# Turning the third and fourth bank of x in 32 by 32 blocks on VectorE and through DRAM

## The chip, the cores and the metric

The kernel runs on one core of a Trainium2 chip. The metric is the device time of one execution in microseconds (us). A core has TensorE (matmuls; the profile calls it PE, and PEld for its weight loads), VectorE (DVE), ScalarE (ACT), GpSimd (POOL) and SyncE (SP), which here only issues DMAs. Each engine works through its own queue in order.

## The reference, cut to what matters

One decoder block on x of 1 x 2048 x 1024 in fp32: a normed and modulated input, one wide projection, two branches (a recurrence and an attention in three window sizes), a merge and an output projection with the residual.

```python
h = rms_norm(x, g_norm[l]) * (1.0 + scale[:, None, :]) + shift[:, None, :]
proj = h @ w_in[l]
x_rnn, z_rnn, q, k, v, z_attn, g_r, g_a = jnp.split(proj, IN_SPLITS, axis=-1)
...
qh = apply_partial_rope(q.reshape(B, S, N_HEADS, HEAD_DIM), cos, sin)
kh = apply_partial_rope(k.reshape(B, S, N_HEADS, HEAD_DIM), cos, sin)
```

The change concerns how h comes to lie with its 1024 features on the partitions, as the matmuls of `proj` want it, for the second half of the rows.

## The kernel before

**Banks and halves.** The 2048 rows are four banks of 512; bank n holds four residues r = 0 to 3 of 128 rows each. Half f = 0 works on banks 0 and 1, half f = 1 on banks 2 and 3. The 1024 features are KT = 8 slices k of 128; KH = 4 slices make one operand half. A bank of x is loaded with rows on partitions (`load_x`, L541: two DMAs of 1 MB, each with two residues), normed (squares with a row sum, a reciprocal root, a scaling), and then *turned*: `turned` (L561) transposes, for one k, the four 128 x 128 pieces on TensorE into a PSUM tile, and `build` (L564) makes from it a high part (L571, ScalarE, with scale and shift by feature) and a low part (L578 and L166 or L169) of an operand. The split into high and low is there because every fp32 product is computed as three fp32r matmuls (L152).

**The products.** Two weight blocks of 128 columns make a pair; for a pair and the two banks of a half, `strassen` (L349) computes seven products of 12 matmuls of 128 x 512 (a *product* below) instead of eight, from sums of weights and sums of operands (B11, B21 from the even bank; B12, B22 from the odd one; T1 to T4 mixed). Their order is X(B11), the previous pair's V(B22), Z(T2), W(T3), V(T1), X(B21), Y(T4). X has two PSUM buffers, Z, W, V and Y one each. The X of a pair is copied by ScalarE to u1 (L385) before X(B21) adds into the same bank; VectorE adds u2 (L386) and u3 (L391) and evicts V and Y with a sum (`total`, L455).

**What sets the order.** Around the change the order on every engine is the order in which the code is written (`tc.manual_schedule()`). `prod` counts the products, and after the matmuls of product n, ahead of its eviction, `run_late` runs what `later(d, fn)` or `steps_after` have registered for it; so "at product d" is a place in the queue of each engine. Weights are loaded (L255, on SP), summed (L284 to L298, VectorE) and split (L160 ScalarE, L166 GpSimd) four products ahead.

**The rotated phase** of a half is the last of its projection: six pairs (rotated q, two plain, rotated k, two plain), 42 products; in the first half it runs from 571.16 to 688.75 us, product 16 at 611.96 us. The evictions there (L1118, L455) are scaled (L1123), rotated on VectorE and GpSimd (L1138, L1142, L1145) and stored to `kqT` by SP (L1150, L1182). In the first half `next_norm` (L1285) loads bank 2 at product 3, squares at 7 to 10 (L1293), takes the root at 11 and 12 (L173, L178 to L182), scales at 14 to 17 (L1297), and `next_even` (L1302) turns and builds its eight k's in the last two pairs. The turned x of bank 3 is made later, in the second half's values stage (`values_half(1)`): the load is issued at its start, `norm_x` (L545) norms it, and `build_odd` (L588) turns and builds B12 (tile b12h, b12l) and B22, then T1 to T4, while TensorE computes the values of bank 2.

## Time and profile before

| | |
|---|---|
| median of 3 runs | 2168.82 us (2168.06 to 2169.25) |
| profiled execution | 2169.86 us |
| its span | 2168.0 us |
| granted TensorE clock, mean | 0.998 |
| TensorE busy | 2138.5 us, 99% |
| VectorE, ScalarE, GpSimd busy | 1495.3, 1295.4, 1111.4 us |
| DMA | 521.39 MB, mean 240 GB/s |

All rows of the profile are of the one profiled execution. A row of a timeline gives the start and the duration in us, the engine, the line, the operation, out<-in by the program's names, shape and count, and in brackets the idle time of that engine just before and what ended it. "SPq" is SyncE's queue issuing DMAs. Matmuls overlap, so what one costs is read from the distance of starts.

### The profile page before, as it was taken

The numbers are of one execution on the slowest core, as the hardware profiler recorded it, in microseconds if no ns is written. First come the engines' busy times: TensorE is split into PE (matmuls) and PEld (weight loads), VectorE is DVE, ScalarE is ACT, GpSimd is POOL, SyncE is SP. The second block draws the span as 40 slices with busy tenths as digits, with TensorE's granted clock in tenths as the row PEclk, the third lists the DMA queues.
The fourth block names the chain that finished last, engine by engine and source line by source line (L and its number), as shares of the span: only waits on it lengthen the run. The fifth ranks groups of instructions, "written<-read, shape, count | busy, mean of one in ns | idle before, by whom it ended". The sixth has DMA issues, their size and how long they took to land.

```text
span 2168.0 us, 32583 instructions
## 1 busy us (share of the span) xinstructions
PE 2138.5 (99%) x10538; PEld 1788.4 (82%) x10539; DVE 1495.3 (69%) x2590; ACT 1295.4 (60%) x2591; POOL 1111.4 (51%) x868
## 2 busy tenths in 40 slices
PE   9999999999999999999999999999999999999998
PEld 6888788888888888888888887888888988878886
DVE  6759877768656725544446584677777787688887
ACT  5748668668644537557547522777877877444333
POOL 1467667677666322223224664466666564422444
PEclk9999999999999999999999999999999999999999
DMA  8467887886655378899996667889886777898553
GB/s 301 144 209 260 278 296 266 284 302 222 175 116 166 113 244 286 294 311 308 326 322 212 161 162 212 279 260 281 263 270 212 244 230 235 298 321 293 181 171 111
DMA packets 416431, 521.39 MB, mean 240 GB/s; under 512 B 107558, under 2 KB 282882, under 8 KB 415236
## 3 DMA queue, kind: packets, MB, share of 16 engines
q1 hardware_dynamic: 376244, 401.65, 59.6%
q10 hardware_dynamic: 34384, 99.78, 12.2%
q0 software_dynamic: 5632, 17.88, 2.5%
q8 instruction: 83, 1.36, 0.2%
q14 instruction: 88, 0.72, 0.1%
HBM read 332.02 MB, written 187.17 MB: 239 GB/s over the span
## 4 chain that ended last, share of the span: by engine, by line
PE 66%; DVE 6%; DMA 5%; ACT 2%; issue 2%; POOL 1%; SPq 0%; POOLq 0%; ACTq 0%; DVEq 0%
PE X L152 13%; PE V L152 13%; PE pj L152 9%; PE Z L152 7%; PE W L152 7%; PE Y L152 6%; PE sc L152 4%; PE o L152 4%; PE pg L152 1%; DMA fg<-mrT 1%; PE pT L1560 1%; DMA fg<-gaT 1%; PE pT L1573 1%; DVE ptl L169 1%; DVE yl L169 1%
## 5 line engine op out<-in xcount | busy, mean ns | idle before, releaser
L166 POOL TENSOR_TENSOR S<-R,S 128x512 fp32r<-128x512 f32 x192 | 295.3, 1545 | 170.1 <-ACT S L160 90.5
L152 PE MATMUL X<-T,S 128*128 128x512 f32 x1344 | 323.9, 390 | 1.5 <-ACT u L385 1.3
L152 PE MATMUL pj<-yh,S 128*128 128x512 f32 x896 | 324.8, 404 | 0.3 <-DVE S L169 0.3
L152 PE MATMUL V<-T,S 128*128 128x512 f32 x1344 | 324.3, 390 | 0.5 <-DVE ev L455 0.5
L152 PEld LDWEIGHTS X<-T,S 128*128 128x128 f32 x1344 | 251.8, 188 | 56.3 <-ACT u L385 2.8
L152 PEld LDWEIGHTS V<-T,S 128*128 128x128 f32 x1344 | 252.0, 188 | 54.4 <-ACT S L160 0.9
L166 POOL TENSOR_TENSOR S<-s,S 128x512 fp32r<-128x512 f32 x116 | 170.4, 1469 | 148.1 <-ACT S L160 112.1
L152 PEld LDWEIGHTS pj<-yh,S 128*128 128x128 f32 x896 | 168.7, 189 | 30.3 <-DVE S L169 1.3
L152 PE MATMUL pj<-yl,S 128*128 128x512 f32 x448 | 176.2, 393 | 0.5 <-POOL yl L166 0.3
L1475 ACT ACTIVATE pp<-pp,st 128x256 f32<-128x256 f32 (+3 forms) x256 | 133.6, 523 | 67.4 <-DVE st L1474 66.1
L160 ACT ACTIVATE S<-s 128x512 fp32r<-128x512 f32 x124 | 77.3, 624 | 143.7 <-DVE s L285 93.2
L152 PE MATMUL W<-T,S 128*128 128x512 f32 x672 | 161.7, 390 | 0.0
L152 PE MATMUL Y<-T,S 128*128 128x512 f32 x672 | 161.6, 390 | 0.0
L152 PE MATMUL Z<-T,S 128*128 128x512 f32 x672 | 161.4, 389 | 0.0
L160 ACT ACTIVATE S<-R 128x512 fp32r<-128x512 f32 x200 | 121.4, 622 | 59.0 <-issue 15.2
L169 DVE TENSOR_TENSOR ptl<-pT,pth 128x384 fp32r<-128x384 f32 (+1 forms) x160 | 97.9, 629 | 76.1 <-ACT pth L160 73.8
L152 PEld LDWEIGHTS W<-T,S 128*128 128x128 f32 x672 | 126.0, 188 | 26.9 <-issue 0.9
L152 PEld LDWEIGHTS Z<-T,S 128*128 128x128 f32 x672 | 126.2, 188 | 26.1
L152 PEld LDWEIGHTS Y<-T,S 128*128 128x128 f32 x672 | 126.1, 188 | 26.1
L974 DVE SCALAR_TENSOR_TENSOR xc<-xr,par,xc 128x512 f32<-128x512 f32 x96 | 103.7, 1080 | 57.2 <-ACT xc L968 54.9
L166 POOL TENSOR_TENSOR s<-R,s 128x512 fp32r<-128x512 f32 x32 | 43.1, 1346 | 189.0 <-ACT s L160 176.4
L1540 ACT ACTIVATE pp<-pp,M 128x256 f32<-128x256 f32 (+3 forms) x256 | 118.0, 523 | 9.9 <-DVE M L1663 9.9
(416 smaller groups left out, 4929.1 us busy)
## 6 DMA issues: line engine op xcount, KB each, us to landing
sD<-S ACTq DMA_DIRECT2D x140, 512.0 KB, 3.7
S<-sD SPq DMA_DIRECT2D x140, 512.0 KB, 5.5
S<-wD SPq DMA_DIRECT2D x82, 512.0 KB, 5.6
R<-in_w_in_dram SPq DMA_DIRECT2D x144, 256.0 KB, 3.4
wD<-s ACTq DMA_DIRECT2D x64, 256.0 KB, 5.6
kraw<-kqT SPq DMA_DIRECT2D x32, 384.0 KB, 5.2
T<-in_w_mod_dram SPq DMA_DIRECT2D x16, 512.0 KB, 9.1
vN<-ev SPq DMA_DIRECT2D x32, 256.0 KB, 2.8
```

Of the source, the lines that this page charges most:

```text
L152: nc.tensor.matmul(o, lhsT=l, rhs=r, start=st, stop=sp, **kw)
L160: nc.scalar.activation(o, i, AF.Copy)
L166: nc.gpsimd.tensor_tensor(o, i, h.bitcast(F32), ALU.subtract)
L169: return nc.vector.tensor_tensor(o, i, h.bitcast(F32), ALU.subtract).ins
L974: nc.vector.scalar_tensor_tensor(xc, xr[:, i : i + CH], cw(i), xc, ALU.mult, ALU.add)
L1475: nc.scalar.activation(pdst, pdst, AF.Exp, bias=m_, scale=-1.0, accum_out=l_)
L1540: nc.scalar.activation(pp, pp, AF.Copy, scale=w)
L1560: nc.tensor.transpose(pt[:, c0 + j * P : c0 + (j + 1) * P], pp[i][:, k * P : (k + 1) * P], ident)
L1573: nc.tensor.transpose(pt[:, c * P : (c + 1) * P], pp[:, half * P : (half + 1) * P], ident)
```

## The change

There is a DRAM scratch `xD`. In the first half's rotated phase `next_banks` replaces `next_norm`: it loads, norms and turns bank 3 (load at product 1, squares at 5 and 6, root at 7 and 8, scaling at 9 and 10, turning at 11 and 12) and then bank 2 (the same steps from product 12: load 12, squares 16 and 17, turning 22 and 23). `turn_rows` turns one k by four VectorE transposes of 128 x 128, which transpose each 32 x 32 block in place in its 4 x 4 grid, into an "hf" tile (two buffers), and stores that to `xD` by SP (256 KB). `load_turned` brings back four k's with four DMAs, so that the blocks come to lie at their transposed places, in runs of 128 numbers. Bank 2 is reloaded at products 25 and 26 and built without TensorE by `next_even`; bank 3 is reloaded at the start of the second half into the tile `hx` and built in `build_odd`, where strided views (`by_window`, `by_class`) undo the order in which the columns lie. `norm_x` for bank 3 in the second half is gone, and so are the 64 TensorE transposes of banks 2 and 3.

```diff
--- before.py
+++ after.py
@@ -117,6 +117,8 @@
     gateD = scratch("gateD", [1, D])
 
     tabD = scratch("tabD", [2, 2, 32, HALF])
+
+    xD = scratch("xD", [2, KT, P, CH])
 
     sD = scratch("sD", [REBUILT * 7, P, 2, KH, P])
 
@@ -578,6 +580,30 @@
             nc.vector.tensor_scalar(hf[:], pv, g, s, ALU.mult, ALU.add)
             (lo_dve if k % 3 == 0 else lo_pool)(hl[:, k % KH, :], hf[:], hh[:, k % KH, :])
 
+    by_class = lambda ap: ap.rearrange("p (r b a) -> p r b a", r=4, b=4)
+    by_window = lambda ap: ap.rearrange("p (b r a) -> p r b a", r=4, b=4)
+
+    def turn_rows(st, xs, n, k):
+
+        w = T(st, [P, CH], F32, "hf", bufs=2)
+        for r in range(4):
+            nc.vector.transpose(w[:].rearrange("p (t r a) -> p r t a", t=4, r=4)[:, r], xs[r][:, k * P : (k + 1) * P])
+        nc.sync.dma_start(xD[n % 2, k], w[:])
+
+    def load_turned(dst, n, kh):
+
+        src = xD[n % 2, kh * KH : (kh + 1) * KH].rearrange("k (b i) (t q) -> t i k b q", b=4, t=4)
+        for t in range(4):
+            nc.sync.dma_start(dst[t * 32 : (t + 1) * 32].rearrange("p k (b q) -> p k b q", b=4), src[t])
+
+    def build_turned(names, k, h, lo):
+
+        hh, hl = (by_class(t[:, k % KH, :]) for t in B[names[k // KH]])
+        g, s = gs[:, k : k + 1], sh[:, k : k + 1]
+        nc.scalar.activation(hh, by_window(h), AF.Identity, bias=s, scale=g)
+        nc.vector.tensor_scalar(h, h, g, s, ALU.mult, ALU.add)
+        lo(hl, by_window(h), hh)
+
     def operand(name):
         B[name] = (slot(), slot())
 
@@ -585,39 +611,43 @@
         for k in ks:
             build(st, ("B11", "B21"), xs, k, first)
 
-    def build_odd(st, xs):
+    def build_odd(st, xs, f):
 
         B["B12"] = (T(st, [P, KH, CH], F32R, "b12h"), T(st, [P, KH, CH], F32R, "b12l"))
         operand("B22")
-        f32 = lambda b, i, k: B[b][i][:, k, :].bitcast(F32)
+        mine, whole = (by_window, by_class) if f else (lambda ap: ap, lambda ap: ap)
+        f32 = lambda b, i, k: whole(B[b][i][:, k, :].bitcast(F32))
         tt = nc.vector.tensor_tensor
-        h = [T(st, [P, CH], F32, "hx", bufs=KT)[:] for _ in range(KT)]
+        h = [xs[:, k, :] if f else T(st, [P, CH], F32, "hx", bufs=KT)[:] for k in range(KT)]
         for k in range(KH):
             for k2 in (k, KH + k):
-                build(st, ("B12", "B22"), xs, k2, keep=h[k2])
+                if f:
+                    build_turned(("B12", "B22"), k2, h[k2], lo_dve)
+                else:
+                    build(st, ("B12", "B22"), xs, k2, keep=h[k2])
             yield
         for name in ("T1", "T2", "T3", "T4"):
             operand(name)
 
         def split(name, k, t):
-            hh, hl = B[name]
-            hi_act(hh[:, k, :], t)
-            lo_dve(hl[:, k, :], t, hh[:, k, :])
+            hh, hl = (whole(b[:, k, :]) for b in B[name])
+            hi_act(hh, mine(t))
+            lo_dve(hl, mine(t), hh)
 
         for k in range(KH):
             h1, h2 = h[k], h[KH + k]
             t = T(st, [P, CH], F32, "t0", bufs=2)[:]
             tt(t, h2, h1, ALU.subtract)
             split("T3", k, t)
-            tt(h1, h1, f32("B11", 0, k), ALU.subtract)
-            tt(h1, h1, f32("B11", 1, k), ALU.subtract)
+            tt(mine(h1), mine(h1), f32("B11", 0, k), ALU.subtract)
+            tt(mine(h1), mine(h1), f32("B11", 1, k), ALU.subtract)
             split("T1", k, h1)
             yield
             tt(h2, h2, h1, ALU.subtract)
             split("T2", k, h2)
             t = T(st, [P, CH], F32, "t0", bufs=2)[:]
-            tt(t, f32("B21", 0, k), h2, ALU.subtract)
-            tt(t, t, f32("B21", 1, k), ALU.add)
+            tt(mine(t), f32("B21", 0, k), mine(h2), ALU.subtract)
+            tt(mine(t), mine(t), f32("B21", 1, k), ALU.add)
             split("T4", k, t)
             yield
 
@@ -880,14 +910,13 @@
             first = wide_values(vx, 0, n0, (0, 1))
             for _ in range(2):
                 next(first)
-            norm_x(vx, xs)
         else:
             for j in range(KH):
                 store_values(vx, 0, n0, j, pv0[j])
             with tc.issue_after(last_copy[0]):
                 norm_x(vx, xs)
             first = ()
-        odd = build_odd(vx, xs)
+        odd = build_odd(vx, xs, f)
         for _ in first:
             next(odd)
         for ws in wide_values(vx, 1, n0, (0, 1), None if f else ws1):
@@ -1282,37 +1311,45 @@
             later(30 + 2 * q, lambda q=q: total(q))
             later(31 + 2 * q, lambda q=q: bias(q))
 
-    def next_norm():
-
+    def next_banks():
+
+        for d, n in ((1, 3), (12, 2)):
+            xs, ss = [], T(xp, [P, 3, 4], F32, "ss", bufs=2)
+
+            def square(r, xs=xs, ss=ss):
+                jk = T(xp, [P, D], BF16, "hf", bufs=2)
+                nc.scalar.activation(jk[:], xs[r], AF.Square, accum_out=ss[:, 0, r : r + 1])
+
+            def scale(r, xs=xs, ss=ss):
+                nc.scalar.activation(xs[r], xs[r], AF.Copy, scale=ss[:, 1, r : r + 1])
+
+            later(d, lambda xs=xs, n=n: xs.extend(load_x(xp, n, "x", 2)))
+            for r in range(4):
+                later(d + 4 + r // 2, lambda r=r, square=square: square(r))
+                later(d + 8 + r // 2, lambda r=r, scale=scale: scale(r))
+            later(d + 6, lambda ss=ss: rstd_first(ss))
+            later(d + 7, lambda ss=ss: rstd_last(ss))
+            for k in range(KT):
+                later(d + 10 + k // 4, lambda xs=xs, n=n, k=k: turn_rows(xp, xs, n, k))
         xs = []
-        later(3, lambda: xs.extend(load_x(xp, 2, "x", 2)))
-        ss = T(xp, [P, 3, 4], F32, "ss")
-
-        def square(r):
-            jk = T(xp, [P, D], BF16, "hf", bufs=2)
-            nc.scalar.activation(jk[:], xs[r], AF.Square, accum_out=ss[:, 0, r : r + 1])
-
-        for r in range(4):
-            later(7 + r, lambda r=r: square(r))
-            later(14 + r, lambda r=r: nc.scalar.activation(xs[r], xs[r], AF.Copy, scale=ss[:, 1, r : r + 1]))
-        later(11, lambda: rstd_first(ss))
-        later(12, lambda: rstd_last(ss))
+
+        def load(kh):
+            xs.append(T(xp, [P, 2, D], F32, "x", bufs=2)[:].rearrange("p a (k j) -> p (a k) j", j=CH))
+            load_turned(xs[kh], 2, kh)
+
+        for kh in range(2):
+            later(25 + kh, lambda kh=kh: load(kh))
         return xs
 
     def next_even():
-
-        def turn(k):
-            px[k] = turned(x0, k, spare=False)
 
         def make(k):
             if k % KH == 0:
                 operand("B21" if k else "B11")
-            build(xp, ("B11", "B21"), x0, k, pt=px.pop(k))
-
-        px = {}
+            build_turned(("B11", "B21"), k, x0[k // KH][:, k % KH, :], lo_dve if k % 3 == 0 else lo_pool)
+
         for k in range(KT):
-            later(min(k + 1 + (k > 0), KT), lambda k=k: turn(k))
-            later(k + 2 + (k > 0), lambda k=k: make(k))
+            later((k + KH) // 2 + 2 if k >= KH else k + 2, lambda k=k: make(k))
 
 
     for x, (key, pieces) in enumerate(pair_order()):
@@ -1324,7 +1361,9 @@
         if f:
             pools.close("xp")
             vx = pools.open("vx", bufs=1)
-            x1 = load_x(hp, 3, "T", 14)
+            x1 = T(vx, [P, KT, CH], F32, "hx")[:]
+            for kh in range(2):
+                load_turned(x1[:, kh * KH : (kh + 1) * KH], 3, kh)
         values_half(f, x1)
         pools.close("vx")
         plain = plain_pairs(f)
@@ -1359,7 +1398,7 @@
             residual_gate(qp)
         else:
             xp = pools.open("xp", side="right", bufs=1)
-            x0 = next_norm()
+            x0 = next_banks()
         for n, _ in enumerate(rotated_pairs(qp, f, *tabs)):
             next(plain)
             if n and f == 0:
```

Line numbers of the changed kernel lie two higher up to `build` and 26 to 39 higher behind it. VectorE's queue at the place of the first burst, before (u, V, t, R are the tiles of the Strassen sums, evictions and weight sums; ss the row sums of bank 2):

```order
L391 TENSOR_TENSOR u_1038_5610<-W_5584,u_1031_5581 128x512
L173 TENSOR_SCALAR ss_5364<-ss_5364 128x4
L1142 TENSOR_TENSOR t_1023_5544<-t_1023_5544,St_5360 128x512
L293 TENSOR_TENSOR R_1011_5477<-R_1008_5456,R_1011_5477 128x512
L455 TENSOR_TENSOR t_1042_5641<-V_5612,u_1038_5610 128x512
```

and now (x_5383 and x_5385 are the two tiles of bank 3, hf a turned k; the last row evicts V):

```order
L393 TENSOR_TENSOR u_1039_5622<-W_5596,u_1033_5593 128x512
L590 STREAM_TRANSPOSE hf_5637<-x_5383 128x4x32 x2
L590 STREAM_TRANSPOSE hf_5637<-x_5385 128x4x32 x2
L590 STREAM_TRANSPOSE hf_5643<-x_5383 128x4x32 x2
L590 STREAM_TRANSPOSE hf_5643<-x_5385 128x4x32 x2
L590 STREAM_TRANSPOSE hf_5649<-x_5383 128x4x32 x2
L590 STREAM_TRANSPOSE hf_5649<-x_5385 128x4x32 x2
L590 STREAM_TRANSPOSE hf_5655<-x_5383 128x4x32 x2
L590 STREAM_TRANSPOSE hf_5655<-x_5385 128x4x32 x2
L1171 TENSOR_TENSOR t_1026_5556<-t_1026_5556,St_5360 128x512
L295 TENSOR_TENSOR R_1014_5482<-R_1009_5457,R_1014_5482 128x512
L457 TENSOR_TENSOR t_1047_5675<-V_5624,u_1039_5622 128x512
```

Eight rows of block transposes stand now between the u3 sum and the eviction of V; another eight follow behind that eviction.

SP's queue there, before:

```order
L255 DMA R_1029_5577<-in_w_in_dram 128x4x32
L1150 DMA kqT<-t_1020_5522 128x1x128 x4
L255 DMA R_1041_5636<-in_w_in_dram 128x4x32 x4
L255 DMA R_1044_5665<-in_w_in_dram 128x4x32 x4
L1150 DMA kqT<-t_1023_5544 128x1x128 x4
```

and now:

```order
L591 DMA xD<-hf_5637 128x512
L591 DMA xD<-hf_5643 128x512
L591 DMA xD<-hf_5649 128x512
L591 DMA xD<-hf_5655 128x512
L1179 DMA kqT<-t_1024_5531 128x1x128 x4
L257 DMA R_1046_5670<-in_w_in_dram 128x4x32 x4
L591 DMA xD<-hf_5689 128x512
L591 DMA xD<-hf_5695 128x512
L591 DMA xD<-hf_5701 128x512
L591 DMA xD<-hf_5707 128x512
L543 DMA x_5713<-in_x_dram 128x2048
L543 DMA x_5715<-in_x_dram 128x2048
```

The stores of the first four k's, then kqT stores and weight loads, then the stores of the other four, and behind them the load of bank 2's x, which takes the two tiles of bank 3.

ScalarE's queue around the copy u1 of product 14's X, before:

```order
L160 ACTIVATE S_1052_5737<-R_1016_5501 128x512
L1297 ACTIVATE x_5428<-x_5428,ss_5364 128x1024
L1123 ACTIVATE t_1053_5740<-t_1053_5740 128x512
L160 ACTIVATE S_1055_5763<-s_1036_5604 128x512
L385 ACTIVATE u_1057_5771<-X_5699 128x512
```

and now:

```order
L162 ACTIVATE S_1063_5792<-R_1021_5510 128x512
L1321 ACTIVATE hf_5810,ss_5365<-x_5713 128x1024
L1321 ACTIVATE hf_5812,ss_5365<-x_5713 128x1024
L1152 ACTIVATE t_1064_5795<-t_1064_5795 128x512
L162 ACTIVATE S_1068_5821<-s_1037_5616 128x512
L387 ACTIVATE u_1070_5829<-X_5756 128x512
L1321 ACTIVATE hf_5846,ss_5365<-x_5715 128x1024
L1321 ACTIVATE hf_5848,ss_5365<-x_5715 128x1024
```

The scaling of bank 2 stood there; the squares of the newly loaded bank 2 stand there now, two ahead of the scaled eviction t and u1, two behind.

## The prediction

> **What bounds the kernel now.** I read the page first for the busy shares and the chain, then the busy times of two stretches, then the timelines of TensorE, VectorE, ScalarE and SyncE (SP) there. "0.2%" below is about what a measurement of this kernel can tell from no change: 4.3 us.
>
> ```profile
> span 2168.0 us, 32583 instructions
> PE 2138.5 (99%) x10538; PEld 1788.4 (82%) x10539; DVE 1495.3 (69%) x2590; ACT 1295.4 (60%) x2591; POOL 1111.4 (51%) x868
> PE 66%; DVE 6%; DMA 5%; ACT 2%; issue 2%; POOL 1%; SPq 0%; POOLq 0%; ACTq 0%; DVEq 0%
> ...
> 571.16:688.75 117.59, 117.59 (x531) 97.36 (x530) 71.15 (x97) 49.55 (x84) 77.13 (x56) 1.00 0.61 155
> 688.75:775.00 86.25, 85.86 (x395) 70.30 (x394) 49.22 (x80) 44.18 (x80) 34.32 (x25) 1.00 0.42 131
> ```
>
> The last two rows give for a stretch its length, then the busy time (and count) of PE, PEld, DVE, ACT, POOL, then granted clock, DMA share, GB/s. The first is the first half's rotated phase, the second the start of the second half, where bank 3 is built now. TensorE is idle for nothing in the first and for 0.39 us in the second, at full clock. So a matmul taken away is worth its whole time, and a wait put in front of a matmul costs its whole time: the other engines are loose on average, but the sum depends on where they gate TensorE.
>
> **What is removed.** 64 transposes on TensorE, 4 to a k:
>
> ```profile
> L561 PE MATMUL pg<-cs,x x32: 270/272/273, 666.4 to 692.1; 128*128 128x128 f32 x32
> L561 PE MATMUL pg<-cs,T x20: 270/272/273, 705.8 to 725.1; 128*128 128x128 f32 x20
> L561 PE MATMUL Y<-cs,T x12: 272/272/276, 705.9 to 725.8; 128*128 128x128 f32 x12
> ...
> 660.92 2.88 PE L152 MATMUL Y<-T,S 128*128 128x512 f32 x12
> 663.64 2.89 PE L152 MATMUL X<-T,S 128*128 128x512 f32 x12
> 666.36 0.60 PE L561 MATMUL pg<-cs,x 128*128 128x128 f32 x4
> 666.72 3.02 PE L152 MATMUL V<-T,S 128*128 128x512 f32 x12
> 669.57 2.88 PE L152 MATMUL Z<-T,S 128*128 128x512 f32 x12
> ```
>
> Matmuls overlap, so the price is what starts are pushed apart. Product to product is 663.64 − 660.92 = 2.72 us; with four transposes between, X to Z takes 669.57 − 663.64 = 5.93, so a group costs 5.93 − 2 × 2.72 = 0.49. Sixteen groups: 16 × 0.49 = 7.8; I take **7.7**, as some of bank 3's groups lie next to others. Nothing else that is removed lies on TensorE's path (bank 3's squares and scaling, ACT and DVE work at 696 to 705 us, run while TensorE is busy).
>
> **What is added in front of TensorE.** Bank 3's rows are now turned by VectorE at products 11 and 12 of the rotated phase, four k's in a burst, and bank 2's at 22 and 23 (a product here is 12 matmuls; product 16 is the first row below). No row shows the 128x128 strided block transpose. The nearest is a 128x512 one, as many elements as a k:
>
> ```profile
> 611.96 2.88 PE L152 MATMUL Z<-T,S 128*128 128x512 f32 x12
> ...
> 617.40 2.88 PE L152 MATMUL V<-T,S 128*128 128x512 f32 x12
> 620.12 2.88 PE L152 MATMUL X<-T,S 128*128 128x512 f32 x12
> ...
> 601.28 0.65 DVE L173 TENSOR_SCALAR ss<-ss 128x4 f32<-128x4 f32 x1
> ...
> 603.05 0.68 DVE L455 TENSOR_TENSOR t<-V,u 128x512 f32<-128x512 f32 x1
> ...
> 604.33 0.16 DVE L180 TENSOR_TENSOR ss<-ss 128x4 f32<-128x4 f32 x1
> ...
> 612.16 0.69 DVE L455 TENSOR_TENSOR t<-V,u 128x512 f32<-128x512 f32 x1 [1.21 <-PE V L152]
> ...
> L1082 DVE STREAM_TRANSPOSE ev<-ev x1: 702/702/702, 282.6 to 282.6; 128x512 f32<-128x512 f32 x1
> ```
>
> g, a k's four transposes: at least the one 0.70; at most 0.70 plus three more small-operation costs of 0.16 (L180), 1.18. I take 0.9, nearer the 0.70 row. Work for 16 k's, 14 us, fits DVE's idle time in the stretch (117.59 − 71.15 = 46); the danger is only its order. Two buffers hold the turned rows, so k2 cannot be turned before k0's store has landed, and everything behind it in DVE's queue waits, the V eviction (L455) among it.
>
> L, a 256 KB store's issue to landing, and X, the x load's:
>
> ```profile
> DMA to landing us min/median/max: 2.5/2.6/2.7
> gaT<-ev SPq DMA_DIRECT2D x32, 256.0 KB, 4.1
> x<-in_x_dram SPq DMA_DIRECT2D x2, 1024.0 KB, 7.7
> xo<-in_x_dram SPq DMA_DIRECT2D x16, 512.0 KB, 4.0
> ...
> 580.30 0.92 SPq L541 DMA_DIRECT2D x<-in_x_dram  x2
> ...
> 597.86 2.48 SPq L1150 DMA_DIRECT2D kqT<-t  x4
> 600.39 4.81 SPq L255 DMA_DIRECT2D R<-in_w_in_dram  x8
> ...
> 586.02 1.05 ACT L1293 ACTIVATE hf<-x 128x1024 bf16<-128x1024 f32 x1
> ```
>
> The first row is tile grT's five 256 KB stores from 440 to 600 us: L 2.7 taken, bounds 2.5 and the 4.1 of gaT's row. X: first x tile, at most 586.02 − 580.30 = 5.7 there; 5.0 taken, bounds 4.0 (half the size, xo) and 7.7.
>
> **Bank 3's burst, step by step.** Start 601.28, where ss is done now. k0 to 602.2, k1 beside its store; k0's store lands 602.2 + 0.1 (handoff) + 2.7 = 605.0. k2, k3 to 606.9. SP then issues their stores, and four kqT stores (2.48) and four weight loads (half of 4.81), 4.9 in all, before k4's store: so k4's store goes out at about 612.25 and lands at 614.95 (k4 itself waited for k2's). k6, k7 to 616.85. Only then may bank 2's x be loaded, since it takes the two buffers that k7 reads: issue 617.3, landed 622.3.
>
> ScalarE is next in the row: the two squares of that x (product 16) stand in its queue ahead of u1, the copy of product 14's X (L385), and product 19 accumulates into the bank that u1 copies, so it must come after.
>
> ```profile
> 612.94 0.63 ACT L1123 ACTIVATE t<-t 128x512 f32<-128x512 f32 x1 [1.68 <-DVE t L455]
> 613.48 0.62 ACT L160 ACTIVATE S<-s 128x512 fp32r<-128x512 f32 x1
> 614.00 0.58 ACT L385 ACTIVATE u<-X 128x512 f32<-128x512 f32 x1
> ```
>
> Squares 2 × 1.04 to 624.4, then those three rows' steps (0.54, 0.52, 0.58) to 626.05 instead of 614.5. Product 19 (X, at 620.12 now) waits for that copy: **S1 = 626.05 − 620.12 = 5.9**. The V evictions late by the same burst (V of product 15 to about 620.5, needed at 617.40) cost 3.1 alone, but lie inside these 5.9, since product 18 then ends before 626.
>
> **Bank 2's burst.** With everything counted from 626.05: scale ends and k0 is turned by +11.0; k0's store lands at +13.9; k2, k3 to +16.0; V of product 22 is evicted by +16.9, and product 25 would start at 6 × 2.72 = +16.3: 0.6. The second four end the same way at +27.2 to +29.8 against product 29 at +27.8: 0 to 2. **S2 = 1.2**.
>
> **What I cost at nothing.** Stores and reloads on SP: 16 × 0.34 and 16 × 0.62 us of issue, SP waits for nothing that TensorE needs within the four products of lead that the weight loads have. Bank 2's turned rows are reloaded at products 25, 26, some 20 us before they are built. Bank 3's reload waits for the old pool to close, so for the last kqT store, and takes eight issues:
>
> ```profile
> 689.70 1.29 SPq L1182 DMA_DIRECT2D kqT<-t  x2
> 748.16 0.64 PE L152 MATMUL V<-S,b12h 128*128 128x512 f32 x2
> ```
>
> That is about 691 + 3 + 8 × 0.62 + 4, some 703; first use of bank 3's operands is 748.16 less bank 3's and the last of bank 2's transposes, 737 or later. Cover after the building: some 18 us. Without it ScalarE stands before the building with its weight splits behind (a rival below).
>
> **Sum.** −7.7 + 5.9 + 1.2 = −0.6. The profiled execution took 2169.86 (span 2168.0, 1.9 around it), so 2169.3; it stood 1.0 over the median of the runs, 2168.82. So **2168.2 us** for the runs: TensorE's gain is spent on waiting for the burst.
>
> [...] The four transposes in TensorE's stream cost 0.49, 0.12 each, against my 0.9 on VectorE (0.22 each). [...]
>
> **Rivals.**
>
> *A, faster: the burst fits.* For: DVE idles 1.2 to 2.1 us at products 15, 16; stores just ahead of this stage took 2.5 to 2.7. With g 0.70, L 2.5, X 4.0, S1 falls by 5 × 0.2 + 2 × 0.2 + 1.0 to 3.5, and S2 to 0: −4.2. If ScalarE's squares also come earlier than I have them, by a weight load less on SP ahead of k4's store, 1 to 3 us more: 2162 to 2164. Against: all must fall on the low side. I put its time at **2163**.
>
> *B, slower: the bursts run at the pace of the stores.* Mechanism: two buffers, each freed only by a landed store; two landings stand on bank 3's chain, two on bank 2's. For: the stretch runs at a DMA share of 0.61, and gaT's 4.1. At L = 4.1: S1 5.9 + 2 × 1.4 = 8.7, S2 1.2 + 2.8 to 5.4, sum +5.0 to +7.6: **2175**. It decides (over +4.3) from L of about 3.8; all high ends (X 7.7, g 1.18 too) give +13, 2182.
>
> *C, slower: the second half waits for bank 3's reload.* The first b12h build stands in ScalarE's queue ahead of weight splits and evictions; if the reload comes 10 us later than 703, these starve TensorE: each us late beyond some 6 costs one, 2172. Against: 0.42 DMA share there.
>
> *D, no change of stalls: the burst never gates* (the buffers prove free in time): then the whole 7.7 shows, 2161.
>
> **How the numbers follow.** Forecast (2164.5 to 2173.1) 0.43, with the rule's g and a mild C in it; A 0.25 and D 0.07, together faster 0.32; B 0.17 and a strong C 0.08, slower 0.25. The forecast's own range, from the terms' bounds one at a time, is 2165 to 2173. For 8 in 10 I go down to 2162.0 (A, most of it) and up to 2175.5 (B at L = 4.1), leaving a tenth on each side.
>
> **What would show it.** Right: no L561 transposes after 660 us; 64 block transposes of about 0.22 us; DVE rows of these with waits of 2 to 3 us ended by the store's DMA; ScalarE idle before the second x's square, ended by that load, and a TensorE X idle of some 6 us ended by the u copy near product 19, a small V wait near 25. Wrong: no such idle time (D), idle over 8 us with stores landing after 3.8 us (B), or TensorE idle between 690 and 750 (C); a block transpose far from 0.22 moves g.

## The result, and the profile after

The changed kernel takes **2194.77 us** (median of 4 runs, 2191.76 to 2196.89) against 2169.03 before in the same session (2168.06 to 2170.89): 1.0118 times as long, 95% interval 1.0106 to 1.0131. The forecast was 2168.2, with a range of 2162.0 to 2175.5. It was wrong: the waits in front of TensorE cost not the 7.1 us that were forecast but some 32 (24.3 more by the spans, and the 7.7 gained). Where they arose is read from the profile first; which step of the prediction failed is told behind the experiments.

The page of the changed kernel, its rows on span and busy time, and its busy times in two stretches (length, then PE, PEld, DVE, ACT, POOL, then granted clock, DMA share, GB/s):

```profile
span 2192.3 us, 32558 instructions
PE 2140.8 (98%) x10474; PEld 1786.3 (81%) x10475; DVE 1506.7 (69%) x2640; ACT 1294.6 (59%) x2584; POOL 1112.9 (51%) x868
...
571.00:690.00 119.00, 103.38 (x436) 83.19 (x435) 72.15 (x152) 49.45 (x84) 62.02 (x45) 0.96 0.73 183
715.00:790.00 75.00, 68.86 (x290) 55.30 (x289) 42.07 (x56) 31.28 (x54) 28.72 (x22) 0.95 0.52 139
```

64 matmul records fewer, as many as transposes were taken out, and yet 24.3 us more. In 119 us of the rotated phase TensorE is idle for 15.6, in the 75 us of the second half's values for 6.1, and in both the granted clock is below 1.00 (0.96 and 0.95); before it was 1.00 in each of the two.

Both kernels run the same matmuls, but for the transposes, and in the same order, but for a few that change places near the seam of two stages. So the n-th matmul of one can be laid beside the n-th of the other; where a kernel's records hold one matmul more, the count is shifted by one. Four such places before (a fifth, product 35 at 663.64, stands in the prediction), from TensorE's timeline: product 11, product 20, and two matmuls of the second half's values:

```profile
598.36 2.88 PE L152 MATMUL V<-T,S 128*128 128x512 f32 x12
...
622.84 2.88 PE L152 MATMUL Y<-T,S 128*128 128x512 f32 x12
...
704.22 1.52 PE L152 MATMUL V<-S,T 128*128 128x512 f32 x6
...
770.48 1.55 PE L152 MATMUL X<-S,T 128*128 128x512 f32 x6
```

The same five places in the changed kernel, and all larger idle times of TensorE between them (in brackets, with what ended them):

```profile
599.18 2.88 PE L154 MATMUL V<-T,S 128*128 128x512 f32 x12
...
612.22 3.02 PE L154 MATMUL V<-T,S 128*128 128x512 f32 x12 [2.00 <-DVE t L457]
...
624.27 4.58 PE L154 MATMUL V<-T,S 128*128 128x512 f32 x12 [3.59 <-DVE t L457]
629.45 3.03 PE L154 MATMUL X<-T,S 128*128 128x512 f32 x12 [0.60 <-ACT u L387]
632.32 2.88 PE L154 MATMUL Y<-T,S 128*128 128x512 f32 x12
...
638.87 3.03 PE L154 MATMUL V<-T,S 128*128 128x512 f32 x12 [0.95 <-DVE t L457]
...
655.53 4.49 PE L154 MATMUL V<-T,S 128*128 128x512 f32 x12 [8.20 <-ACT S L162]
...
684.35 3.05 PE L154 MATMUL X<-T,S 128*128 128x512 f32 x12
...
722.10 1.52 PE L154 MATMUL V<-S,T 128*128 128x512 f32 x6
...
735.09 2.93 PE L154 MATMUL Z<-S,T 128*128 128x512 f32 x6 [4.66 <-ACT ev L887]
...
741.61 3.03 PE L154 MATMUL X<-S,T 128*128 128x512 f32 x12 [1.04 <-ACT ev L887]
...
793.12 1.52 PE L154 MATMUL X<-S,T 128*128 128x512 f32 x6
```

The change of the distance from place to place says where the time went. 0.8 us had come before product 11. Then:

| stretch (before's clock) | after | of it |
|---|---|---|
| product 11 to 20 (598.36 to 622.84) | +8.7 | first burst (bank 3) |
| product 20 to 35 (to 663.64) | +11.2 | second burst (bank 2) |
| product 35 to the values (to 704.22) | −2.8 | bank 2's transposes gone, −3.9 |
| the values of bank 2 and 3 (to 770.48) | +4.8 | bank 3's transposes gone, −3.8; so the waits cost +8.6 |
| to the end | +1.6 | +1.9 at the start of the attention, some −0.3 behind it |

The last 1.9 us stand near 1350 us, where TensorE idles for 1.25 us before and 1.62 after (in the changed kernel at 1373 us, and the granted clock is 0.50 there from 1375.60 to 1378.95 us). In the experiments this place gave −0.7 to +3.6 us without order, so that it is left out of the comparisons by stretch.

**What the bursts wait for.** VectorE's block transposes as a group, and the stores' time from issue to landing (groups by line; idle time of VectorE in us and times):

```profile
L590 DVE STREAM_TRANSPOSE hf<-x x64: 263/269/314, 605.7 to 660.0; 128x128 f32<-128x128 f32 x64
  DMA xD<-hf: 12.9, 5
DMA to landing us min/median/max: 2.0/2.0/2.8
```

VectorE's and SP's timelines of the changed kernel (the SP rows are issues), ahead of and around both bursts:

```profile
587.57 0.01 DVE L1167 LOAD_MASK_SELECT t<-t  x1 [3.81 <-ACT t L1152]
...
605.67 1.65 DVE L590 STREAM_TRANSPOSE hf<-x 128x128 f32<-128x128 f32 x8
608.73 1.66 DVE L590 STREAM_TRANSPOSE hf<-x 128x128 f32<-128x128 f32 x8 [1.41 <-DMA xD<-hf]
...
612.09 1.65 DVE L590 STREAM_TRANSPOSE hf<-x 128x128 f32<-128x128 f32 x8
618.50 1.67 DVE L590 STREAM_TRANSPOSE hf<-x 128x128 f32<-128x128 f32 x8 [4.75 <-DMA xD<-hf]
...
623.44 0.68 DVE L457 TENSOR_TENSOR t<-V,u 128x512 f32<-128x512 f32 x1
...
635.47 0.69 DVE L286 TENSOR_TENSOR s<-R,R 128x512 f32<-128x512 f32 x1 [5.35 <-DMA R<-in_w_in_dram]
...
646.26 1.09 DVE L590 STREAM_TRANSPOSE hf<-x 128x128 f32<-128x128 f32 x5 [0.73 <-ACT x L1324]
652.55 1.67 DVE L590 STREAM_TRANSPOSE hf<-x 128x128 f32<-128x128 f32 x8 [5.20 <-DMA xD<-hf]
654.14 0.65 DVE L300 TENSOR_TENSOR s<-R,s 128x512 f32<-128x512 f32 x1
```

```profile
610.79 2.50 SPq L1179 DMA_DIRECT2D kqT<-t  x4
613.34 2.26 SPq L257 DMA_DIRECT2D R<-in_w_in_dram  x4
615.69 4.82 SPq L591 DMA_DIRECT2D xD<-hf  x4
620.60 0.89 SPq L543 DMA_DIRECT2D x<-in_x_dram  x2
...
646.15 1.18 SPq L1211 DMA_DIRECT2D kqT<-t  x2
647.43 1.14 SPq L257 DMA_DIRECT2D R<-in_w_in_dram  x2
648.68 1.25 SPq L1211 DMA_DIRECT2D kqT<-t  x2
650.02 4.54 SPq L591 DMA_DIRECT2D xD<-hf  x4
```

A block transpose of 128 x 128 takes 0.27 us, a k of four 0.83 (1.65 for eight), and a store lands in 2.0. Neither is slow. But k4 was turned at 612.9, and its store went out at 615.69, behind eight other issues of SP; the second bank's k0 was turned at 646.5 and its store went out at 650.02. With two buffers k6 of bank 3 and k2 of bank 2 wait for that, and with them all that stands behind on VectorE: the eviction of V (623.44 in the first burst), and at 654.14 the weight sum L300 that product 25 needs.

ScalarE's timeline of the changed kernel, at four places: the first square of bank 3 with the wait for its x, the square that waits for bank 2's x and the u1 copy behind it, the weight split that product 25 waited for, and the first builds of bank 3 with the first eviction of the values:

```profile
584.81 1.06 ACT L1321 ACTIVATE hf<-x 128x1024 bf16<-128x1024 f32 x1 [4.30 <-DMA x<-in_x_dram]
...
625.68 1.06 ACT L1321 ACTIVATE hf<-x 128x1024 bf16<-128x1024 f32 x1 [2.39 <-DMA x<-in_x_dram]
...
628.82 0.57 ACT L387 ACTIVATE u<-X 128x512 f32<-128x512 f32 x1
...
654.88 0.63 ACT L162 ACTIVATE S<-s 128x512 fp32r<-128x512 f32 x1 [7.61 <-DVE s L300]
...
723.69 2.94 ACT L603 ACTIVATE b12h<-hx,mod,gs 128x512 fp32r<-128x512 f32 x4 [8.80 <-DMA hx<-xD]
...
734.46 0.58 ACT L887 ACTIVATE ev<-Z 128x512 f32<-128x512 f32 x1
```

The first row explains why the first burst came late. SP issued the load of bank 3's x at 576.65; the square of product 5 waited 4.30 us for it and could begin 8.2 us after that issue. The scaled eviction L1152 stood behind the square (at 586.91, before the change 582.96), and VectorE's shuffle waited 3.81 us for that (587.57, before 583.63; so 3.1 late, beyond the 0.8). The operations of bank 3's root, which now stand ahead of the burst too, keep VectorE busy there for some 3 us, and it made nothing up: the burst began 3.6 us later than the same place before. How the lateness divides between the two no run shows.

All eight builds and four weight splits stand now ahead of the eviction of Z. In the values stage the order is not that of the code, but a scheduler's. Before, the builds were paced by the transposes on TensorE and the eviction (at 707.38) came ahead of the first of them.

### The profile page after: what moved, and what is told of

Same layout as the page of the kernel before. It is cut to its first block, busy times and chain, and to the rows that moved or that the text cites. A ratio compares the mean times of both kernels' runs of the same rounds, so it can differ in the third digit from the quotient of the medians.

```text
span 2192.3 us, 32558 instructions
## 1 busy us (share of the span) xinstructions
PE 2140.8 (98%) x10474; PEld 1786.3 (81%) x10475; DVE 1506.7 (69%) x2640; ACT 1294.6 (59%) x2584; POOL 1112.9 (51%) x868
## 4 chain that ended last, share of the span: by engine, by line
PE 62%; DVE 7%; DMA 5%; issue 3%; POOL 2%; ACT 2%; SPq 1%; POOLq 0%; ACTq 0%; DVEq 0%
PE X L154 12%; PE V L154 11%; PE pj L154 11%; PE Z L154 6%; PE W L154 6%; PE Y L154 5%; PE sc L154 4%; PE o L154 4%; PE pg L154 1%; PE pT L1599 1%; POOL S L168 1%; PE pT L1612 1%; DMA meT<-fg 1%; DVE ptl L171 1%; DVE pp L1513 1%
```

## The experiments

Theory T, formed from these traces: the new work is cheap, but it is put where an in-order queue has something urgent behind it: VectorE's bursts behind stores, the stores behind SP's other issues, the evictions of the values behind builds that wait for a reload. Rival M: the extra work and traffic (14 us on VectorE, 16 transfers of 256 KB each way) slow the phase in whatever order. Two more theories come up on the way: S, that SP's queue is what holds the stores up, and P, that the place in the phase where a bank is turned decides. The other letters are the rivals named in each expectation.

The table gives for each kernel how much longer (+) or shorter (−) the stretches of the table above are than before, from one profiled execution each, and the ratio of the runs with its 95% interval. "11 to 35" holds both bursts. Equal code differs there by up to 2.6 us between executions: the stretch from product 11 to 20 is the same code in the change, e2 and e3 and took 8.7, 11.3 and 11.2 us more.

| kernel | 11 to 35 | 35 to values | values | ratio |
|---|---|---|---|---|
| the change | +19.9 | −2.8 | +4.8 | 1.0118 (1.0106 to 1.0131) |
| e1_spread | +12.6 | −3.1 | +7.8 | 1.0086 (1.0071 to 1.0101) |
| e2_evfirst | +21.8 | −3.9 | −0.2 | 1.0110 (1.0093 to 1.0127) |
| e3_bank3only | +11.2 | 0.0 | −1.0 | 1.0058 (1.0043 to 1.0073) |
| e4_bank2only | +2.0 | −0.6 | +1.1 | 1.0018 (1.0008 to 1.0027) |
| e5_actq | +24.0 | −3.9 | +2.8 | 1.0115 (1.0098 to 1.0132) |
| e6_spread_actq | +5.1 | −2.5 | +5.7 | 1.0041 (1.0027 to 1.0056) |
| e7_all | +5.0 | −0.9 | +3.2 | 1.0026 (1.0015 to 1.0037) |
| e8_bank3only_fixed | +0.9 | 0.0 | −4.7 | 0.9987 (0.9978 to 0.9997) |
| e9_all_early | +8.4 | +4.8 | −1.4 | 1.0053 (1.0038 to 1.0068) |
| e10_all_early_actload | +8.8 | −0.3 | +0.5 | 1.0044 (1.0029 to 1.0059) |
| e11_b3_lateload | +0.8 | 0.0 | −4.7 | 0.9991 (0.9981 to 1.0001) |
| e12_b3_spqueue | +5.7 | +1.8 | −2.9 | 1.0022 (1.0012 to 1.0031) |
| e13_b2_alone | 0.0 | −3.9 | −0.4 | 0.9987 (0.9978 to 0.9996) |
| e14_b3_again | +0.4 | 0.0 | −4.9 | 0.9991 (0.9983 to 1.0000) |
| e15_both_swapped | +0.9 | +2.3 | −0.2 | 1.0021 (1.0012 to 1.0031) |

### One bank alone, as the change does it

e3: bank 3 by the new way, bank 2 (loaded at product 12) back on TensorE; the core of the edit:

```diff
-            for k in range(KT):
+            for k in range(KT if n == 3 else 0):
                 later(d + 10 + k // 4, lambda xs=xs, n=n, k=k: turn_rows(xp, xs, n, k))
...
-            build_turned(("B11", "B21"), k, x0[k // KH][:, k % KH, :], ...)
+            build(xp, ("B11", "B21"), x0, k, pt=px.pop(k))
```

> Edit: bank 3 alone goes the new way (turned at products 11 and 12 as in the changed kernel); bank 2 is loaded at 12, normed, and then turned by TensorE and built as before the change. Theory T: first burst 8.5 and second half 7.7 stay, the second burst's 11.3 go, bank 3's transposes (3.8) are saved, bank 2's are not: 2169 + 8.5 + 7.7 - 3.8 = 2181. Rival M (each bank costs half of the loss of phase and traffic): 2169 + 13 = 2182 with idle time spread, and the halves would show it: no single stall of over 3 us at products 15 to 19. Rival Q (bank 2's burst is the harm, bank 3's alone is harmless): 2168 to 2173.

e4: bank 2 by the new way at the same products, bank 3 back on TensorE in the second half.

```diff
-        for d, n in ((1, 3), (12, 2)):
+        for d, n in ((12, 2),):
...
-            x1 = T(vx, [P, KT, CH], F32, "hx")[:]
-            for kh in range(2):
-                load_turned(x1[:, kh * KH : (kh + 1) * KH], 3, kh)
+            x1 = load_x(hp, 3, "T", 14)
```

> Edit: bank 2 alone goes the new way, at the same products as in the changed kernel (load 12, turned 22 and 23, reload 25 and 26); bank 3 is loaded, normed and turned by TensorE in the second half as before the change. Theory T: its x is no longer late, but the burst still stands on its own stores, which stand behind kqT stores and weight loads in SP's queue (4.4 us there in the changed kernel): 3 to 8 us of TensorE idle time near products 24 to 27, 3.9 saved, nothing in the second half: 2168 to 2174. Rival Q2 (only the lateness handed on by the first burst made the second one costly): under 1 us of idle time, 2165 to 2166.

e3 took 2182.15 us (2180.3 to 2183.25), e4 2174.74 (2170.68 to 2177.82), against 2169.83 before. Bank 3's burst costs its 11.2 us by itself, in single stalls of 1.9 to 2.8 us, and by product 20 the whole loss of the phase is over. Q, with 2173 at most, falls. T's 2181 is met by luck in its parts: the burst cost 11.2 instead of 8.5 and the start of the second half, −1.0 where −3.8 was due, 2.8 instead of 7.7. Nor does e3 separate T from M, which gave 2182 with no stall over 3 us (though its idle time was to be spread, and the stalls end by product 19); e8 below does.

Bank 2's burst costs 2.0 when its x is not late, less than T's 3 to 8 and more than Q2's 1, and its gain does not come, −0.6 where −3.9 was due. TensorE's timeline of e4 has a second wait, at product 35, that ends with the low part of a weight split on GpSimd; VectorE's timeline has what is behind it:

```profile
642.24 2.98 PE L154 MATMUL V<-T,S 128*128 128x512 f32 x12 [1.78 <-ACT S L162]
...
672.29 2.56 PE L154 MATMUL X<-T,S 128*128 128x512 f32 x10 [2.13 <-POOL S L168]
...
668.09 0.01 DVE L1168 LOAD_MASK_SELECT t<-t  x1 [6.58 <-DMA kqT<-t]
```

GpSimd's operation on t at 668.93 waited 5.03 us for this shuffle, the split stood behind it, and the shuffle waited for a kqT store that SP issued only at 663.81, behind the eight reloads of bank 2 (650.12 to 658.29) and four weight loads. It is the shared queue again, with the reloads in place of the stores.

By the 2.0 of e4, of the 11.2 us at the second burst of the changed kernel some 9 were handed on by the first one.

### The second half's order

e2: the builds of bank 3 behind the four evictions of bank 2's first values.

```diff
         for _ in first:
-            next(odd)
-        for ws in wide_values(vx, 1, n0, (0, 1), None if f else ws1):
-            next(odd)
+            if not f:
+                next(odd)
+        for x, ws in enumerate(wide_values(vx, 1, n0, (0, 1), None if f else ws1)):
+            with tc.issue_after(last_ev[0]):
+                for _ in range((2, 2, 1, 1)[x] if f else 1):
+                    next(odd)
```

> Edit: in the second half the builds of bank 3's operands are issued behind the four evictions of bank 2's first values, two steps at a time; the rotated phase is left as in the changed kernel. Theory T (the builds, which wait for the reload, were put ahead of four evictions and the weight splits in ScalarE's queue): the 4.66 and 1.04 us of TensorE idle time and the half clock after them go, 2194.8 - 7.7 = 2187. Rival L (the reload itself is late for the products of bank 3): TensorE waits some 10 us later for b12h or T1 to T4 instead, 2192 to 2196.

2193.75 us (2189.17 to 2196.86): by the runs 1 us less than the change, a time in L's range. The trace does not show L's mechanism, though: TensorE waits nowhere for bank 3's operands, and the values went from +4.8 to −0.2, 5.0 of the 8.6 us. The profiled execution is the fastest of the four, 2189.17; where the others lost more is not known. So T holds for the place, its size was put 2.7 us too high, and the total of the runs does not show it (the two intervals overlap). In e8 below, which has the same edit, nothing is lost there.

### The burst and the queue

e1: bank 3 one k a product, bank 2 two, later.

```diff
-        for d, n in ((1, 3), (12, 2)):
+        for d, n, per in ((1, 3, 1), (18, 2, 2)):
...
-                later(d + 10 + k // 4, lambda xs=xs, n=n, k=k: turn_rows(xp, xs, n, k))
+                later(d + 10 + k // per, lambda xs=xs, n=n, k=k: turn_rows(xp, xs, n, k))
...
-            later(25 + kh, lambda kh=kh: load(kh))
+            later(32 + kh, lambda kh=kh: load(kh))
```

> Edit: the same work, but bank 3's k's are turned one to a product (products 11 to 18) and bank 2's two to a product (28 to 31; its load, squares, root and scaling move to 18, 22, 24, 26; its reload to 32 and 33). Theory T (the two buffers and the in-order queues: a burst of four k's stands on landed stores with an eviction or a weight sum queued behind it): the 8.5 us lost at the first burst and the 11.3 at the second go to under 1.5 together, the 7.7 at the start of the second half stay, so 2194.8 - 18 = 2175 to 2178. Rival M (VectorE's 14 us of extra work and the 16 MB of extra traffic slow the phase whatever their order): at least 8 us of TensorE idle time stay between products 11 and 35, 2183 or more.

2189.34 us (2183.74 to 2190.35). T's expectation fell: 12.6 us are still lost, and M seemed to be right. But VectorE's idle time before the transposes was still nearly all for stores (the changed kernel had 12.9):

```profile
  DMA xD<-hf: 9.9, 6
```

Hence theory S: with the burst gone a store still waits for its turn in SP's queue, behind kqT stores and weight loads of 0.6 us each. e5 changes the queue alone:

```diff
-        nc.sync.dma_start(xD[n % 2, k], w[:])
+        nc.scalar.dma_start(xD[n % 2, k], w[:])
```

> Edit: the changed kernel with one word changed: the stores to xD are issued by ScalarE's queue, not by SP's. Theory S (a store waits in SP's queue behind kqT stores and weight loads at 0.6 us each, and these wait for VectorE in turn; only then two buffers are too few): VectorE's wait before k6 of bank 3 falls from 4.75 to under 2.2, that before k2 of bank 2 from 5.20 to under 2.5, the phase loses 10 to 14 us instead of 19.9, 2184 to 2189. Rival B (two buffers are too few for a burst of four, wherever the store is issued): over 17 us are still lost in the phase, 2192 or more.

e6 is e1 and e5 together.

> Edit: as e1_spread (bank 3 one k a product, bank 2 two), with the stores on ScalarE's queue. Theory S: with neither burst nor SP's queue nothing of VectorE waits over 1 us for a store; of e1_spread's 12.5 us lost in the phase under 3 are left, the second half's 8.8 stay: 2189.3 - 10 = 2178 to 2181. Rival M (extra work and traffic): over 8 us are still lost in the phase, 2184 or more.

e5 took 2195.24 us (2193.39 to 2199.84), e6 2180.15 (2177.91 to 2181.72). For the loss between products 11 and 35 this makes a square:

| | stores on SP's queue | stores on ScalarE's queue |
|---|---|---|
| four k's a product | 19.9 (the change) | 24.0 (e5) |
| one or two k's a product | 12.6 (e1) | 5.1 (e6) |

Neither edit does it alone. e6 is in S's range for the time, though 5.1 us are left of the phase's loss where under 3 was expected. In e5, ScalarE's in-order queue waits for the burst, and its weight splits with it; this is e5's group of transposes, what VectorE waited for and who waited for VectorE:

```profile
  DMA xD<-hf: 11.8, 7
...
  ACT S L162: 16.6, 2
```

So S as it was put for e5 (the queue alone, 10 to 14 us) fell to its rival B; the pair of both holds. The same question for bank 3 alone, which is the cleaner one, is answered by e8 and e12 below.

e7 is e6 with e2's edit.

> Edit: e6_spread_actq and e2_evfirst together (spread turning, stores on ScalarE's queue, builds of bank 3 behind the evictions). Theory S with T: phase under 3 us lost, second half 1 lost, 7.7 saved: 2164 to 2170. Rival M: 2172 or more.

2176.82 us (2174.22 to 2181.26): M's side of the line (2172) by the number. 5.0 us are left in the phase, 4.4 of them behind product 20, where bank 2 is turned two k's a product; the values take 3.2 more, where −3.8 was due. Two causes were suspected: that bank 2 is turned among the rotated pair's evictions, and that SP issues bank 3's eight reloads (5.6 us) ahead of six weight loads of the values. The first falls with e9 and e15; the second stays untested, as e9 and e11 show.

### Which version gains

e8: bank 3 alone, one k a product, stores on ScalarE's queue, builds behind the evictions: e3 with the edits of e1, e5 and e2, and bank 2 loaded at 19.

> Edit: bank 3 alone goes the new way, one k to a product from 11 to 18, stores on ScalarE's queue, builds behind the evictions; bank 2 (loaded at 19) is turned by TensorE as before the change. Theory S with T: phase under 2 us lost, second half 1, 3.8 saved: 2167 to 2170. Rival M: half of the loss of e1_spread's phase is still there, 6 us: 2172 or more.

2168.3 us (2165.78 to 2170.13) against 2171.35 before. Between products 11 and 770 us TensorE has no idle time worth a row, the phase loses 0.9, and the values gain 4.7: bank 3's transposes (3.8), the 0.39 of idle time that stood there before, and half a microsecond that no row names. T with S holds, M falls: the work and the traffic of a bank cost TensorE 0.9 us at most. VectorE's wait for stores in e8:

```profile
  DMA xD<-hf: 1.1, 1
```

e12: e8 with the stores back on SP's queue, still one k a product.

> Edit: e8_bank3only_fixed with the stores back on SP's queue (still one k a product). Theory S (the queue decides once the burst is gone): the phase loses some 8 to 9 us at products 15 to 22 as in e1_spread, 2176 to 2179. Rival (in e1_spread bank 2's part did it): under 2 us lost, 2168 to 2170.

2175.66 us (2170.73 to 2177.58), 5.7 us lost in the phase and 7.4 us of waits for stores:

```profile
  DMA xD<-hf: 7.4, 4
```

The queue decides once the burst is gone: 4.9 us of the phase (less than the 8 to 9 expected), and up to 770 us 8.4 in all, with the 1.8 and 1.8 of the two stretches behind it. The runs agree: against before, e12 is 0.35%, 7.6 us, longer than e8.

e11: e8 with the reload of bank 3 issued behind the first two weight loads of the values.

```diff
             for _ in range(2):
                 next(first)
+            for kh in range(2):
+                load_turned(xs[:, kh * KH : (kh + 1) * KH], 3, kh)
```

> Edit: e8_bank3only_fixed with bank 3's reload issued behind the first two weight loads of the values stage. Theory P: e8 shows no TensorE idle time between 560 and 800 us, so nothing is left to win there: within 0.1% of e8, 2167 to 2169 with before at 2170. Rival: the weights of the values come earlier and a hidden loss goes, 1 to 2 us faster.

2168.25 us (2164.56 to 2170.36) against 2169.94, as expected the same as e8. But it tests nothing: by the two traces SP issues in the same order in e8 and e11, the eight reloads behind two weight loads and ahead of five, so the edit left the order on SP as it was. e11 counts as a repetition of e8. e14 is e8 once more:

> The kernel of e8_bank3only_fixed once more, in five rounds: by its trace it is 3.9 us shorter from product 11 to the attention than before the change, so 0.9975 to 0.9990. Rival: the gain of e8 was a lucky draw, interval holding 1.

2168.62 us (2165.23 to 2170.29) against 2169.78. The interval ends at 1.0000, so that e14 by itself does not exclude its rival. By the traces the kernel is 4 to 5 us shorter between product 11 and 770 us; of the runs it can be said that three measurements (e8, e11 and e14) gave 0.9987, 0.9991 and 0.9991, a gain of 2 to 3 us at the edge of what they can tell.

e13: bank 2 alone, loaded at 3, squared from 7, turned one k a product at 13 to 20, in the plain pairs; stores and reload on ScalarE's queue.

```diff
-        for d, n in ((1, 3), (12, 2)):
+        for d, n in ((3, 2),):
...
+                later(13 + k, lambda xs=xs, n=n, k=k: turn_rows(xp, xs, n, k))
...
-            later(25 + kh, lambda kh=kh: load(kh))
+            later(28 + kh, lambda kh=kh: load(kh))
```

> Edit: bank 2 alone goes the new way, at the best place found for bank 3: loaded at product 3, turned one k a product at 13 to 20 (plain pairs), stores and the reload (28, 29) on ScalarE's queue; bank 3 as before the change. Theory S with P (queue and place are all): under 1.5 us lost in the phase, 3.9 saved: 2166 to 2169 with before at 2170. Rival R (the reload and its landing cost by themselves, as the 2 us before X at some 672 in e4, e9 and e10, after POOL): 2 to 3 us lost near product 37, no gain: 2169 to 2171.

2167.09 us (2165.34 to 2169.6) against 2169.78, 0.9987 (0.9978 to 0.9996): nothing is lost in the phase and the whole 3.9 us of bank 2's eight groups come. At this place, with the reload on ScalarE's queue, it costs nothing, and R falls here. (In e10 below it does not quite: behind the reloads four kqT stores took 6.6 to 7.1 us to land, where 2.1 is the median; VectorE's shuffle waited 4.51 us for them, and TensorE 2.42 us at product 35.)

e9, e10 and e15 try both banks. e9: as e7, with bank 3 turned two k's a product at 10 to 13, bank 2 two a product at 23 to 26, reload at 28. e10: e9 with bank 2's reload on ScalarE's queue.

> Edit: both banks the new way, with stores on ScalarE's queue and builds behind the evictions as in e7_all, and two times moved: bank 3 turned two k's a product at 10 to 13, bank 2 loaded at 13, squared at 18, turned two a product at 23 to 26 (ahead of the rotated k pair's shuffles instead of in them), reloaded at 28 and 29; bank 3's reload is issued behind the first two weight loads of the values stage. Theory P (place: e7_all loses 5 us because bank 2's turning falls among the rotated pair's evictions, and 4.5 because SP issues eight reloads ahead of the values' weights): under 2 us lost in the phase, under 1 after it, 7.7 saved: 2162 to 2166. Rival N (two k's a product are too many for two buffers anywhere): 3 to 6 us lost at products 12 to 27: 2168 to 2173.

> Edit: e9_all_early with the reload of bank 2 on ScalarE's queue too. Theory P: within 1 us of e9_all_early, as SP's eight issues (5 us) lie inside the four products of lead. Rival (the weights' loads behind those eight issues are late, as X at 672 after POOL S suggested in e4_bank2only, 2.1 us): 2 us faster than e9_all_early.

2181.74 us (2179.73 to 2183.11) and 2179.73 (2179.22 to 2180.04): worse than e7, so theory P is wrong in its place part. Two k's a product in the plain pairs cost 3.6 to 3.9 us before product 20, where one a product costs 0 to 0.9 (e7, e8, e13): that is rival N's mechanism, though the times lie above N's 2173 too. P's other part was not tested: in e9's trace, too, SP issues bank 3's reloads ahead of the five weight loads. e10's reload on the other queue is 2 us faster, as its rival said, though the two intervals touch. By the traces it saves some 5 us from product 35 to the values, where in e9 VectorE waits 7.83 us for kqT stores that SP issues behind the eight reloads, and TensorE 5.70; 2 of the 5 are lost again in the values.

e15: bank 2 first, one a product at 11 to 18, then bank 3, one a product at 28 to 35, in the rotated pair's evictions; bank 2's reload at 36, since bank 3 has the two x tiles until then.

> Edit: both banks, bank 2 first: turned one k a product at 11 to 18; bank 3 loaded at 18 and turned one k a product at 28 to 35, in the rotated k pair's evictions; bank 2 reloaded at 36 and 37 and built from 40 on, three products later than before; stores and bank 2's reload on ScalarE's queue, builds of bank 3 behind the evictions. Theory P (place): 2 to 4 us lost at products 28 to 37 and up to 2 at the start of the second half where bank 2's builds are late, 7.7 saved: 2166 to 2170. Rival (one k a product is harmless anywhere once SP is left alone): under 2 us lost, 2163 to 2165.

2175.5 us (2172.03 to 2177.3), above both expectations. The phase loses 0.9, all of it before product 20: one k a product is harmless among the rotated evictions too, and P's place part falls a second time. With both banks' work and stores in the phase this speaks against M once more. The loss moves behind product 35 (+2.3, where −3.9 was due) and to the values (−0.2, where −3.8 was due). That the late reload and builds cause it fits the rows, but no run shows it:

```profile
682.35 3.01 PE L154 MATMUL X<-T,S 128*128 128x512 f32 x12 [2.20 <-ACT u L387]
697.34 2.76 PE L154 MATMUL V<-S,T 128*128 128x512 f32 x7 [1.78 <-DVE t L457]
```

So each bank alone gains 2 to 3 us, and no version with both does. More buffers for the turned rows, which would have been the plainest test of the two buffers, were not tried; how much of the bursts' cost two buffers alone cause stays open.

## Why the prediction was wrong, point by point

**The gain of 7.7 us: right.** Eight groups of bank 2 give −3.9 in e2, e5 and e13, bank 3's −3.8 and what idle time was left there −4.7 to −4.9 in e8, e11 and e14.

**g and L: right, on the good side.** A k takes 0.83 us against 0.9 (bounds 0.70 to 1.18), a store 2.0 (median) to 2.8 against 2.7, below the bound of 2.5 that was set. One transpose has 0.27 us in the median and 0.31 at the longest of the 64, but four in a row take 0.83, 0.21 each, as they overlap. The "rule's g" that the chance of the forecast also takes in is a price that no run shows; the 0.83 stands in its place. Rival B (stores that land after 3.8 us and more) did not come about; the time is lost although the stores are fast.

**S1 = 5.9: the mechanism right, 2.8 us too small.** The chain went as written: k2 behind k0's store, k6 behind k4's store behind eight issues of SP, then the x load (620.60, landed 625.68: 5.1 against 5.0), the square, u1 at 628.82, product 19 at 629.45. What was mis-sized is the first term: the burst began not at 601.28 but at 605.67 (0.8 of that had come before). The start was taken from a row of before, at the place that the small ss operation had there. But VectorE was 3.6 us later by then, since bank 3's own x was late and the root's operations stood ahead: the text asked for the landing of bank 2's x and not for that of bank 3's (8.2 us, beyond the bound of 7.7). The sign that was named, an X idle of some 6 us, showed as 0.60, since V had waited 2.00 and 3.59 us before it and product 18 ran in part at half clock (0.50 from 624.63 to 628.04 us): the same 8.7 us, in other places.

**S2 = 1.2: wrong, 11.2.** The step "counted from 626.05, k0 is turned by +11.0; its store lands at +13.9" failed twice; the +11.0 was set without its terms. From 629.45 on k0 was turned at +17.1, since the weight sum L286, which stands ahead of the root's operations, waited for a load that SP had issued late (635.47, idle 5.35). And the store was issued 3.5 us after that, behind SP's other work. The text had counted SP's issues ahead of the store in the first burst and not in the second. And it had asked only for the eviction of V behind the burst; the weight sum L300 and with it the split and product 25 stood behind it as well: TensorE idled 8.20 us there.

**"SP waits for nothing that TensorE needs within the four products of lead", cost nothing: wrong**, and this is the step behind it. It added up SP's new issues and compared them with the lead, not with the order of SP's queue. There the stores of turned rows stand behind kqT stores and weight loads (eight issues, 4.9 us, ahead of k4's), and what is behind them stands still while they wait for VectorE (11 times, 16.3 us, from 600 to 660 us), which waits in turn for a store to land (5 times, 12.9 us). e12 prices this for one bank, with all else equal to e8: 4.9 us in the phase, 8.4 up to 770 us. With bursts the queue is not the whole of it: in e5, with the stores off SP's queue, the phase lost 24.0.

**Bank 3's reload, cost nothing, and rival C at 8%: wrong, 8.6 us.** The landing was put at 703; with the 17.9 us that were lost before, that is some 721, and the builds began at 723.69. So it was not the landing that was wrong. The 18 us of cover were counted to the first matmul that reads bank 3; the eviction of Z, which now stood behind the builds on ScalarE, was due much earlier (707.38 before, some 725 with what was lost). Rival C named this queue and gave it too little: with the transposes gone nothing paced the builds any more, and the scheduler of that stage put all eight ahead of four evictions. e2 and e8 show it: with the evictions first the stretch goes from +4.8 to −0.2 and −4.7 (e8 has other edits besides). e2 shows 5.0 of the 8.6; of the rest, waits for evictions of 1.50, 0.40 and 1.67 us stay in e2, and no run shows what causes them.

**The chances.** A, B and C were weighed as alternatives. In truth three waits added up, each in a queue of its own, and a late first burst made the second later: e4 has 2.0 where the change has 11.2.

## What to carry to other kernels

A transfer or a transpose that is taken off the bounding engine must be priced at its place in the order of every queue it enters: list what is behind it (sums and splits of weights as well as evictions), and what stands ahead of its DMA on the issuing queue, for each burst anew. For one bank, small doses with the stores off SP's queue cost 0.9 us at most here; both banks in bursts on SP's queue cost 20, and for them neither remedy alone was enough. And where a scheduler sets the order, taking away the work that paced a stage can move what was in step ahead of what is urgent.

## What the runs showed of the hardware

**The clock dropped after some short waits.** A product takes 2.88 us by its rows; behind some waits it takes 4.6, 1.7 more, which is 3.4 us at half speed. The granted clock agrees: in the changed kernel it was 0.50 from 624.63 to 628.04 us, inside product 18 (the 4.58 us from 624.27), and 1.00 on both sides; in e3, with two such products, its mean was 0.97 over the 119 us from 571 to 690 us. It happened behind 3.59 and 8.20 us in the changed kernel, but not behind 2.00, and in e3 behind less, while a wait of 1.88 had the usual length:

```profile
614.20 4.60 PE L154 MATMUL V<-T,S 128*128 128x512 f32 x12 [2.75 <-DVE t L457]
626.14 3.01 PE L154 MATMUL V<-T,S 128*128 128x512 f32 x12 [1.88 <-DVE t L457]
631.56 4.61 PE L154 MATMUL X<-T,S 128*128 128x512 f32 x12 [2.42 <-ACT u L387]
```

In e1 a wait of 2.42 us left the speed as it was (the product took 2.98), one of 2.74 did not (4.58). In e7 even 3.31 us (at 661.91) left it (3.00), and in e15 1.78 us (at 697.34, in the rows of e15) were enough: seven matmuls took 2.76 us, where seven take 1.75 before, and the granted clock was 0.93 from 690 to 715 us. So between 1.8 and 3.3 us the length of a wait alone does not tell, and no run shows what else decides. Where the clock dropped, the product took up to 1.7 us more (4.61 in e3 against 2.88). Behind the 8.20 us it was 0.50 for 6.8 us, from 651.95 to 658.75, the first 3.6 of them while TensorE still waited.

**Half speed cost nothing inside another wait.** In the first burst the half clock of product 18 lies inside the wait for u1, which lasts 0.60 us longer than the product, so it cost nothing of its own there; behind the 8.20 us it cost 1.6 (4.33 us from start to start, 655.53 to 659.86, against 2.72).
